# A two-layer hybrid attention kernel: the memory keys normed from unscaled rows, only the values scaled

## The chip, the cores and the metric

The kernel runs on one core of a Trainium2 chip. The metric is the time of one execution on the device in microseconds (us); the lower the better. The core has TensorE (PE: matrix products and transpositions; its weight loads have a row of their own, PEld), VectorE (DVE), ScalarE (ACT), GpSimd (POOL) and SyncE (SP), whose queue issues nearly all transfers here.

## The reference

Two layers, each with 256 tokens of 1024 columns. In each layer the tokens are normed and projected; three kinds of attention run (causal over one block, 6 heads; dilated, 6 heads; over 256 rows of a memory, 4 heads); each output is gated, and one projection brings all back to 1024 columns. What the change touches is the memory's side:

```python
def rms_norm(x, g):
    xf = x.astype(jnp.float32)
    y = xf * lax.rsqrt(jnp.mean(xf * xf, axis=-1, keepdims=True) + EPS)
    return (y * g.astype(jnp.float32)).astype(x.dtype)
...
    mkv = jnp.einsum('bmd,de->bme', rms_norm(mem, mem_norm_g), w_mem_kv)
    m_k, m_v = jnp.split(mkv, 2, axis=-1)
    qm = rms_norm(to_heads(m_q, N_HEADS_MEM), qk_g[4])
    km = rms_norm(to_heads(m_k, N_HEADS_MEM), qk_g[5])
    om = from_heads(memory_attention(qm, km, to_heads(m_v, N_HEADS_MEM)))
```

The factor r = rsqrt(mean(mem²) + EPS) of a memory row is one number for the row, so it may be put on after the projection; and a key's own norm, over the 64 columns of a head, is taken of the row with r in it.

## The kernel before

All weights come in fp32 and are split into two parts, `hi` (a cast on ScalarE) and `lo` (raw less `hi`, on VectorE); a product is three matrix products (`hi`·`xmh`, `hi`·`xml`, `lo`·`xmh`), added in PSUM. Each weight arrives in a `raw` tile (3 buffers), and each piece of it becomes one `hi` and one `lo` (5 buffers of each). The projections follow one another on TensorE in a written order: memory keys and values (`mkv`), memory queries (`mq`), their gate (`mg`), then the dilated heads' `bq`, `bk`, `bv` and so on. Each projection has two accumulators of PSUM, `acc`, in a ring of four: `bq` takes the two that `mq` had, so its second accumulator is free only when VectorE has read the second row of `mq` (the product by the gain in `normed`, line 266).

Attention runs as tasks beside the projections: a planner on the host writes each task's TensorE instructions between those of the projections by planned times, and that order is fixed. The first task on TensorE transposes one pair of memory heads (`qn` and `kn`, 128 rows of tokens and of memory at a time: q0, k0, q1, k1, line 113) in the middle of `bq`, after five of its eight steps.

`normed` is the norm of heads: squares on ScalarE (`sq`, 260), their sums on VectorE (`hss`, 262), mean plus EPS on VectorE (`ms`, 154), the power of -1/2 on GpSimd (`hrs`, 155), the product by the gain (`t1`, 266) and by the norm (276), both on VectorE. `row_scale` gives a row's factor: squares of 1024 columns with their sum on ScalarE (160), `ms` on VectorE, the power on GpSimd.

In layer 0 `mkv` ends before the factors `rmem` are there. So the rows are copied out of PSUM unscaled (`kv`, 561); the squares of memory row tile 0 follow in the middle of `mq` (564), those of tile 1 after `mq`'s norm (568); and each row tile of keys and values (512 columns) is scaled in place on ScalarE (573) before the keys' norm (574). A row tile here is 128 memory rows. Layer 1 has the factors at hand and scales in the copy.

Within an engine, the instructions of this part stand in an order that a scheduler settles when the program is built, from planned times; on the chip each engine then goes through its own list in that order.

Of the kernel before, what the change touches and what calls it, by code (L numbers as in the profile page):

```python
# [10 lines left out]
F32 = mybir.dt.float32  # L11
F32R = mybir.dt.float32r
AF = mybir.ActivationFunctionType
ALU = mybir.AluOpType
AX = mybir.AxisListType

P = 128
T = 256
NT = T // P
D = 1024  # L20
KD = D // P
HD = 64
# [44 lines left out]
def hybrid_kernel(ctx: ExitStack, tc: tile.TileContext, x, mem, mem_t, gains, w_in, w_out, w_mem_kv, qk_g, const, out):  # L67
    nc = tc.nc
    cp = ctx.enter_context(tc.tile_pool(name="cp", bufs=1))
    wp = ctx.enter_context(tc.tile_pool(name="wp", bufs=2))  # L70
    sp = ctx.enter_context(tc.tile_pool(name="sp", bufs=2))
# [17 lines left out]
    def pin(ins):  # L89

        return tc.keep_in_program_order(ins) if pinning[0] else ins

    memT = cp.tile([P, KD, T], F32, name="memT")
    mem_sb = cp.tile([P, NT, D], F32, name="mem_sb")
# [29 lines left out]
    def poll():  # L124

        for task in list(tasks):
            if task[0] <= clock[0]:
                try:
                    task[0] = next(task[1]) + clock[0]
                except StopIteration:  # L130
                    tasks.remove(task)
# [20 lines left out]
    def rsqrt(dst, ss, n, scale):  # L152
        ms = sp.tile([P, n], F32, tag="ms", name="ms", bufs=4)
        pin(nc.vector.tensor_scalar(ms, ss, scale, EPS, op0=ALU.mult, op1=ALU.add))  # L154
        pin(nc.gpsimd.tensor_tensor(dst, ms, mhalf[:, :n], op=ALU.pow))  # L155

    def row_scale(src, t, name, junk):

        ss = sp.tile([P, 1], F32, tag="ss", name="ss", bufs=4)
        pin(nc.scalar.activation(junk, src[:, t], AF.Square, accum_out=ss))  # L160
        r = sp.tile([P, 1], F32, tag=name, name=name, bufs=2)
        rsqrt(r, ss, 1, 1.0 / D)
        return r
# [26 lines left out]
    gB = cp.tile([P, DEPTH, 6, HD], F32, name="gB")  # L190

    def load_gains(a, b):
        pin(nc.sync.dma_start(gB[:, :, a:b], bass.AP(tensor=qk_g.tensor, offset=qk_g.offset + a * HD,
                                                     ap=[[0, P], [6 * HD, DEPTH], [HD, b - a], [1, HD]])))
# [57 lines left out]

    def heads(v):
        return v.rearrange("p (h d) -> p h d", d=HD)

    def normed(acc, n, dst, tables):

        h = n // HD
        sq = sp.tile([P, n], F32, tag="sq", name="sq", bufs=2)
        pin(nc.scalar.activation(sq, acc, AF.Square))  # L260
        ss = sp.tile([P, h], F32, tag="hss", name="hss", bufs=4)
        pin(nc.vector.tensor_reduce(ss, heads(sq), axis=AX.X, op=ALU.add))  # L262
        rs = sp.tile([P, h], F32, tag="hrs", name="hrs", bufs=4)
        rsqrt(rs, ss, h, 1.0 / HD)
        t1 = sp.tile([P, n], F32, tag="t1", name="t1", bufs=2)
        pin(nc.vector.tensor_tensor(heads(t1), heads(acc), tables[0][:, None, :].to_broadcast([P, h, HD]),
                                    op=ALU.mult))
        if len(tables) > 1:
            t2 = sq
            half = dict(s=2, d=HD // 2)  # L270
            pin(nc.vector.tensor_tensor(t2.rearrange("p (h s d) -> p h s d", **half),
                                        acc.rearrange("p (h s d) -> p h s d", **half)[:, :, ::-1, :],
                                        tables[1].rearrange("p (s d) -> p s d", s=2)[:, None]
                                        .to_broadcast([P, h, 2, HD // 2]), op=ALU.mult))
            pin(nc.vector.tensor_tensor(t1, t1, t2, op=ALU.add))
        pin(nc.vector.tensor_tensor(heads(dst), heads(t1), rs.unsqueeze(2).to_broadcast([P, h, HD]), op=ALU.mult))  # L276
# [97 lines left out]
    for i, (l, c) in enumerate(order):  # L374
        if c in e_rows:
            e0, n = e_rows[c]
            units += [(i, a, min(2, n - a), D) for a in range(0, n, 2)]
        else:
            n = 512 if c == "mkv" else in_cols[c][1]
# [101 lines left out]
    for l in range(DEPTH):  # L481
# [3 lines left out]
        if l == 0:  # L485
# [4 lines left out]
            r_mem = []  # L490
# [44 lines left out]
        def head_tiles(n, nv):  # L535
            return [sp.tile([P, NT, n], F32, tag=c, name=c, bufs=1) for c in ("qn", "kn")] + [
                sp.tile([P, NT, nv], F32, tag="v", name="v", bufs=2),
                sp.tile([P, n // P, T], F32, tag="gate", name="gate", bufs=2)]
# [14 lines left out]
        qn, kn, kv, gate = head_tiles(256, 512)  # L553
        v = kv[:, :, 256:512]
        ready = dict(gate=1e9)
        mq, steps = project(xs, weights(), 256)
        for i, _ in enumerate(steps):
            poll()
            if i == 0:
                for t in range(NT):  # L560
                    pin(nc.scalar.activation(kv[:, t], mkv[t], AF.Copy, **(dict(scale=r_mem[t]) if r_mem else {})))
            if i == 3 and l == 0:
                mem_junk = sp.tile([P, D], F32, tag="v", name="mem_junk", bufs=2)
                r_mem.append(row_scale(mem_sb, 0, "rmem", mem_junk))
        for t, acc in enumerate(mq):
            normed(acc, 256, qn[:, t], [gB[:, l, 4]])
        if l == 0:
            r_mem.append(row_scale(mem_sb, 1, "rmem", mem_junk))
            pin(nc.sync.dma_start(cst, const))
            load_gains(0, 4)  # L570
        for t in range(NT):
            if l == 0:
                pin(nc.scalar.activation(kv[:, t], kv[:, t], AF.Copy, scale=r_mem[t]))
            normed(kv[:, t, 0:256], 256, kn[:, t], [gB[:, l, 5]])
        pinning[0] = False
        start_heads(2, 6, qn, kn, None, v, gate, ready, D_NORM + D_MEM)
        tab = prepare_tables(l)
# [3 lines left out]
        for kind, e0 in ((2, 3), (0, 0)):  # L581
# [7 lines left out]
            qn, kn, v, gate = head_tiles(384, 384)  # L589
# [75 lines left out]
```

## Time and profile before

| | |
|---|---|
| time, median of 3 runs | 294.21 us (294.15 to 294.81) |
| the profiled execution's own time | 294.36 us |
| its span, first to last instruction | 292.6 us |
| TensorE busy | 285.8 us, 98% of the span |
| VectorE busy | 204.3 us, 70% |
| ScalarE busy | 200.0 us, 68% |
| GpSimd busy | 53.8 us, 18% |
| granted clock of TensorE | 1.000 in the mean |

The 1.76 us between the span and the time of that execution lie outside what the profile shows. A busy share is a mean over the whole span; where an engine stands idle for a moment is read from the views below.

### The profile page before, as it was taken

The page shows a single profiled execution, that of the slowest core. Times are in us where ns is not written, and L with a number is a line of the kernel's source. Part 1 is how long each engine was busy: PE and PEld are TensorE (multiplying, and loading weights), DVE is VectorE, ACT ScalarE, POOL GpSimd, SP SyncE. Part 2 cuts the span into 40 slices and gives each one's busy share as a digit, 9 for nine tenths or more (in the row PEclk, how much of TensorE's full clock was granted, in tenths as well). Part 3 has the DMA queues.
Part 4 walks back from the last instruction along what each step waited for, and adds up shares of the span by engine and source line. Part 5 has one row for each costly group of instructions (what it writes and reads, how often), then busy time and mean ns, then how long its engine had stood idle before and what let it go on. Part 6 is the DMA issues. An engine that isn't in the chain of part 4 may idle for free.

```text
span 292.6 us, 4974 instructions
## 1 busy us (share of the span) xinstructions
PE 285.8 (98%) x1810; PEld 250.6 (86%) x1810; DVE 204.3 (70%) x456; ACT 200.0 (68%) x445; POOL 53.8 (18%) x73
## 2 busy tenths in 40 slices
PE   8999889999999999999999999999999999999994
PEld 5699879889988999877788999989899899987773
DVE  1696889796557997755585577979655699765413
ACT  2997858785798747978375655868588864698600
POOL 0103596030002130000011049703000123000000
PEclk9999999999999999999999999999999999999999
DMA  7999565609227046646106727560913715820003
GB/s 236 389 367 373 184 182 186 179 2 319 57 71 237 19 155 262 196 162 224 65 19 233 225 101 195 168 179 2 298 38 109 239 52 165 316 81 36 3 0 143
DMA packets 32793, 47.33 MB, mean 162 GB/s; under 512 B 1280, under 2 KB 27648, under 8 KB 32768
## 3 DMA queue, kind: packets, MB, share of 16 engines
q1 hardware_dynamic: 32336, 46.22, 48.5%
q10 hardware_dynamic: 432, 0.79, 0.8%
q8 instruction: 14, 0.23, 0.3%
q14 instruction: 11, 0.09, 0.1%
HBM read 45.96 MB, written 1.05 MB: 161 GB/s over the span
## 4 chain that ended last, share of the span: by engine, by line
PE 86%; DMA 7%; DVE 3%; POOL 1%; issue 1%; ACT 1%; SPq 0%; DVEq 0%; ACTq 0%
PE acc L110 68%; PE wk L113 7%; PE wk L110 5%; PE o L110 5%; DMA raw<-in_w_in_dram 3%; DMA x_sb<-in_x_dram 2%; DVE lo L430 1%; DMA raw<-in_w_mem_kv_dram 1%; POOL hrs L155 1%; DVE hss L262 0%; ACT xn L160 0%; POOL r L155 0%; DVE ms L154 0%; DVE kn L276 0%; ACT hi L429 0%
## 5 line engine op out<-in xcount | busy, mean ns | idle before, releaser
L430 DVE TENSOR_TENSOR lo<-raw,hi 128x768 fp32r<-128x768 f32 (+1 forms) x91 | 97.4, 1089 | 34.1 <-ACT hi L429 33.4
L429 ACT CAST hi<-raw 128x768 fp32r<-128x768 f32 (+1 forms) x91 | 83.8, 937 | 31.2 <-PE acc L110 22.7
L110 PE MATMUL acc<-hi,xmh 128*128 128x384 f32 (+2 forms) x252 | 67.3, 349 | 0.8 <-ACT hi L429 0.8
L110 PE MATMUL acc<-hi,xml 128*128 128x384 f32 (+2 forms) x252 | 63.6, 335 | 0.0
L110 PE MATMUL acc<-lo,xmh 128*128 128x384 f32 (+2 forms) x252 | 63.6, 335 | 0.0
L155 POOL TENSOR_TENSOR hrs<-ms,mhalf 128x6 f32<-128x6 f32 (+1 forms) x24 | 30.1, 1255 | 121.2 <-DVE ms L154 120.8
L110 PEld LDWEIGHTS acc<-hi,xmh 128*128 128x128 f32 x252 | 42.7, 189 | 6.3 <-issue 3.0
L110 PEld LDWEIGHTS acc<-lo,xmh 128*128 128x128 f32 x252 | 45.0, 188 | 1.2
L110 PEld LDWEIGHTS acc<-hi,xml 128*128 128x128 f32 x252 | 44.9, 188 | 1.2
L110 PE MATMUL acc<-hi,yT 128*128 128x512 f32 x128 | 41.0, 402 | 0.0
L110 PE MATMUL acc<-xmh,hi 128*128 128x256 f32 x128 | 29.7, 293 | 0.0
L340 ACT ACTIVATE pr<-pr,nm 128x128 f32<-128x128 f32 (+1 forms) x48 | 21.4, 447 | 11.1 <-DVE nm L338 10.9
L110 PE MATMUL acc<-xmh,lo 128*128 128x256 f32 x128 | 28.4, 283 | 0.0
L110 PE MATMUL acc<-xml,hi 128*128 128x256 f32 x128 | 28.4, 283 | 0.0
L110 PEld LDWEIGHTS acc<-hi,yT 128*128 128x128 f32 x128 | 23.0, 188 | 4.9 <-issue 0.7
L346 ACT ACTIVATE pr<-pr,rinv 128x128 f32<-128x128 f32 (+1 forms) x64 | 25.8, 462 | 0.2 <-DVE rinv L344 0.2
L110 PE MATMUL acc<-lo,yT 128*128 128x512 f32 x64 | 25.0, 391 | 0.0
L110 PEld LDWEIGHTS acc<-xmh,hi 128*128 128x128 f32 x128 | 20.9, 191 | 0.7 <-issue 0.7
L110 PEld LDWEIGHTS acc<-xml,hi 128*128 128x128 f32 x128 | 21.0, 191 | 0.0
L110 PEld LDWEIGHTS acc<-xmh,lo 128*128 128x128 f32 x128 | 21.0, 191 | 0.0
L357 ACT COPY pT<-wk 128x384 f32<-128x384 f32 (+1 forms) x32 | 15.5, 504 | 5.1 <-PE wk L113 5.1
L338 DVE CUSTOM_DVE_ANT_0 pr<-wk,cst 128x128 f32<-128x128 f32 (+1 forms) x48 | 14.2, 352 | 3.0 <-PE wk L110 3.0
(76 smaller groups left out, 355.3 us busy)
## 6 DMA issues: line engine op xcount, KB each, us to landing
raw<-in_w_in_dram SPq DMA_DIRECT2D x24, 768.0 KB, 4.8
raw<-in_w_in_dram SPq DMA_DIRECT2D x7, 1024.0 KB, 5.4
raw<-in_w_out_dram SPq DMA_DIRECT2D x6, 1024.0 KB, 4.9
raw<-in_w_in_dram SPq DMA_DIRECT2D x6, 512.0 KB, 3.7
raw<-in_w_out_dram SPq DMA_DIRECT2D x4, 512.0 KB, 4.2
raw<-in_w_mem_kv_dram SPq DMA_DIRECT2D x2, 1024.0 KB, 5.3
raw<-in_w_mem_kv_dram SPq DMA_DIRECT2D x2, 512.0 KB, 6.5
x_sb<-in_x_dram SPq DMA_DIRECT2D x2, 512.0 KB, 6.7
```

Of the source, the lines that this page charges most:

```text
L110: pe(nc.tensor.matmul(out, a, b, start=start, stop=stop), us)
L113: pe(nc.tensor.transpose(out, a, ident), 0.109)
L155: pin(nc.gpsimd.tensor_tensor(dst, ms, mhalf[:, :n], op=ALU.pow))
L338: nc.vector.tensor_tensor_reduce(out=pr[:, spans[t]], in0=s[:, spans[t]], in1=masks[t], scale=-1.0, scalar=3e38, op0=ALU.add, op1=ALU.min, ...
L340: nc.scalar.activation(pr[:, spans[t]], pr[:, spans[t]], AF.Exp, scale=-1.0, bias=nm[:, t:t + 1], accum_out=sums[:, t:t + 1])
L346: nc.scalar.activation(pr[:, spans[t]], pr[:, spans[t]], AF.Copy, scale=rinv[:, t:t + 1])
L357: nc.scalar.copy(pT[:, :n], ps[:, :n])
L429: pin(nc.scalar.copy(hi, raw))
L430: pin(nc.vector.tensor_tensor(lo, raw, hi.bitcast(F32), op=ALU.subtract))
```

## The change

In layer 0 the keys are normed from the unscaled rows. Right after the copy out of PSUM, ScalarE squares the keys' 256 columns of both row tiles and VectorE sums them (`head_squares`); the two row tiles' own squares (1024 columns each) follow at once. The norm's end, `normed_keys`, forms r²/64 (`r2`), puts it into `ms` as the factor of the sums, and multiplies the unscaled keys by r and by the gain in one instruction. The two scalings in place take the values' 256 columns alone. Layer 1 is as before.

```diff
+    def head_squares(acc, n):
+        sq = sp.tile([P, n], F32, tag="sq", name="sq", bufs=2)
+        pin(nc.scalar.activation(sq, acc, AF.Square))
+        ss = sp.tile([P, n // HD], F32, tag="hss", name="hss", bufs=4)
+        pin(nc.vector.tensor_reduce(ss, heads(sq), axis=AX.X, op=ALU.add))
+        return ss
+
+    def normed_keys(acc, ss, r, dst, table):
+        h = 256 // HD
+        r2 = sp.tile([P, 1], F32, tag="r2", name="r2", bufs=2)
+        pin(nc.vector.tensor_scalar(r2, r, r, 1.0 / HD, op0=ALU.mult, op1=ALU.mult))
+        rs = sp.tile([P, h], F32, tag="hrs", name="hrs", bufs=4)
+        rsqrt(rs, ss, h, r2)
+        t1 = sp.tile([P, 256], F32, tag="t1", name="t1", bufs=2)
+        pin(nc.vector.scalar_tensor_tensor(heads(t1), heads(acc), r, table[:, None, :].to_broadcast([P, h, HD]),
+                                           op0=ALU.mult, op1=ALU.mult))
+        pin(nc.vector.tensor_tensor(heads(dst), heads(t1), rs.unsqueeze(2).to_broadcast([P, h, HD]), op=ALU.mult))
...
             if i == 3 and l == 0:
+                k_ss = [head_squares(kv[:, t, 0:256], 256) for t in range(NT)]
                 mem_junk = sp.tile([P, D], F32, tag="v", name="mem_junk", bufs=2)
-                r_mem.append(row_scale(mem_sb, 0, "rmem", mem_junk))
+                r_mem += [row_scale(mem_sb, t, "rmem", mem_junk) for t in range(NT)]
         for t, acc in enumerate(mq):
             normed(acc, 256, qn[:, t], [gB[:, l, 4]])
         if l == 0:
-            r_mem.append(row_scale(mem_sb, 1, "rmem", mem_junk))
             pin(nc.sync.dma_start(cst, const))
             load_gains(0, 4)
         for t in range(NT):
             if l == 0:
-                pin(nc.scalar.activation(kv[:, t], kv[:, t], AF.Copy, scale=r_mem[t]))
-            normed(kv[:, t, 0:256], 256, kn[:, t], [gB[:, l, 5]])
+                normed_keys(kv[:, t, 0:256], k_ss[t], r_mem[t], kn[:, t], gB[:, l, 5])
+                pin(nc.scalar.activation(v[:, t], v[:, t], AF.Copy, scale=r_mem[t]))
+            else:
+                normed(kv[:, t, 0:256], 256, kn[:, t], [gB[:, l, 5]])
```

The scheduler orders each engine's list anew. TensorE's and SyncE's lists stay the same. The list of ScalarE from the copies out of PSUM on, before (a number behind a name tells buffers apart; `acc_260` and `acc_261` are the two rows of `mq`, `raw_262` and `raw_305` the first and second half of `bq`'s weights):

```order
L561 ACTIVATE v_258<-acc_127 128x512
L561 ACTIVATE v_258<-acc_128 128x512
L160 ACTIVATE mem_junk_298,ss_299<-mem_sb_84 128x1024
L429 CAST hi_307<-raw_262 128x768
L260 ACTIVATE sq_335<-acc_260 128x256
L260 ACTIVATE sq_346<-acc_261 128x256
L160 ACTIVATE mem_junk_298,ss_357<-mem_sb_84 128x1024
L573 ACTIVATE v_258<-v_258,rmem_301 128x512
L429 CAST hi_410<-raw_262 128x768
L260 ACTIVATE sq_366<-v_258 128x256
L429 CAST hi_440<-raw_305 128x768
```

And with the change:

```order
L581 ACTIVATE v_258<-acc_127 128x512
L581 ACTIVATE v_258<-acc_128 128x512
L259 ACTIVATE sq_298<-v_258 128x256
L259 ACTIVATE sq_302<-v_258 128x256
L160 ACTIVATE mem_junk_306,ss_307<-mem_sb_84 128x1024
L160 ACTIVATE mem_junk_306,ss_313<-mem_sb_84 128x1024
L449 CAST hi_321<-raw_262 128x768
L280 ACTIVATE sq_349<-acc_260 128x256
L280 ACTIVATE sq_360<-acc_261 128x256
L594 ACTIVATE v_258<-v_258,rmem_309 128x256
L594 ACTIVATE v_258<-v_258,rmem_315 128x256
L449 CAST hi_414<-raw_262 128x768
L449 CAST hi_444<-raw_319 128x768
```

The keys' squares and both rows' squares now stand ahead of the first cast of `bq`'s weights, and behind it stand the queries' squares and the two scalings of values.

The list of VectorE around the second row of `mq`, before; the product `t1_354<-acc_261` is what frees the second accumulator of `bq`:

```order
L262 TENSOR_REDUCE hss_348<-sq_346 128x4
L154 TENSOR_SCALAR ms_351<-hss_348 128x4
L266 TENSOR_TENSOR t1_354<-acc_261,gB_95 128x256
L430 TENSOR_TENSOR lo_411<-raw_262,hi_410 128x768
L276 TENSOR_TENSOR qn_256<-t1_354,hrs_350 128x256
L154 TENSOR_SCALAR ms_360<-ss_357 128x1
L262 TENSOR_REDUCE hss_368<-sq_366 128x4
L430 TENSOR_TENSOR lo_441<-raw_305,hi_440 128x768
```

And with the change, where that product is `t1_368<-acc_261`:

```order
L282 TENSOR_REDUCE hss_362<-sq_360 128x4
L450 TENSOR_TENSOR lo_415<-raw_262,hi_414 128x768
L154 TENSOR_SCALAR ms_365<-hss_362 128x4
L286 TENSOR_TENSOR t1_368<-acc_261,gB_95 128x256
L450 TENSOR_TENSOR lo_445<-raw_319,hi_444 128x768
L296 TENSOR_TENSOR qn_256<-t1_368,hrs_364 128x256
```

The second `lo` of `bq`, which stood behind that product, now stands ahead of it, and the third `lo` ahead of the norm's end `qn`.

The list of VectorE from there to the end of the second key row, before (`gate` are the two products of `mg`'s gate):

```order
L430 TENSOR_TENSOR lo_441<-raw_305,hi_440 128x768
L154 TENSOR_SCALAR ms_371<-hss_368 128x4
L266 TENSOR_TENSOR t1_374<-v_258,gB_95 128x256
L533 SCALAR_TENSOR_TENSOR gate_259<-th_468,acc_408 128x256
L276 TENSOR_TENSOR kn_257<-t1_374,hrs_370 128x256
L262 TENSOR_REDUCE hss_380<-sq_378 128x4
L533 SCALAR_TENSOR_TENSOR gate_259<-th_471,acc_409 128x256
L154 TENSOR_SCALAR ms_383<-hss_380 128x4
L266 TENSOR_TENSOR t1_386<-v_258,gB_95 128x256
L430 TENSOR_TENSOR lo_481<-raw_305,hi_480 128x768
L276 TENSOR_TENSOR kn_257<-t1_386,hrs_382 128x256
```

And with the change:

```order
L268 TENSOR_SCALAR r2_373<-rmem_309 128x1
L553 SCALAR_TENSOR_TENSOR gate_259<-th_472,acc_412 128x256
L154 TENSOR_SCALAR ms_376<-hss_300,r2_373 128x4
L272 SCALAR_TENSOR_TENSOR t1_379<-v_258,rmem_309,gB_95 128x256
L553 SCALAR_TENSOR_TENSOR gate_259<-th_475,acc_413 128x256
L274 TENSOR_TENSOR kn_257<-t1_379,hrs_375 128x256
L268 TENSOR_SCALAR r2_383<-rmem_315 128x1
L450 TENSOR_TENSOR lo_485<-raw_319,hi_484 128x768
L154 TENSOR_SCALAR ms_386<-hss_304,r2_383 128x4
L272 SCALAR_TENSOR_TENSOR t1_389<-v_258,rmem_315,gB_95 128x256
L450 TENSOR_TENSOR lo_503<-raw_442,hi_502 128x768
L274 TENSOR_TENSOR kn_257<-t1_389,hrs_385 128x256
```

The keys' sums `hss` have left this stretch, two `r2` of one column have come in, and the first `lo` of `bk` (`lo_503`, before `lo_499`) now stands ahead of the last `kn`.

## Rows read from the trace of the kernel before

**Rows 1.** The page's first line: the span of the profiled execution.
```profile
span 292.6 us, 4974 instructions
```

**Rows 2.** All waits of TensorE: engine, line, releaser, us in total, times, longest.
```profile
PE warm L120 <- DVE mhalf L83: 1.0, 1, 1.0
PE wk L113 <- DVE kn L276: 0.9, 1, 0.9
PE acc L110 <- ACT hi L429: 0.8, 1, 0.8
PE acc L110 <- DVE whole L495: 0.4, 1, 0.4
```

**Rows 3.** Timeline of TensorE: start us, us, engine, line, operation, tiles, count, idle before.
```profile
30.91 0.34 PE L110 MATMUL acc<-hi,xmh 128*128 128x384 f32 x1
32.01 0.41 PE L110 MATMUL acc<-hi,xmh 128*128 128x384 f32 x1 [0.77 <-ACT hi L429]
...
37.11 0.27 PE L113 MATMUL wk<-ident,qn 128*128 128x128 f32 x1
...
37.33 0.27 PE L113 MATMUL wk<-ident,qn 128*128 128x128 f32 x1
38.55 0.33 PE L113 MATMUL wk<-ident,kn 128*128 128x128 f32 x1 [0.95 <-DVE kn L276]
```

**Rows 4.** Timeline of VectorE from 27.96 to 45 us.
```profile
27.96 0.96 DVE L430 TENSOR_TENSOR lo<-raw,hi 128x768 fp32r<-128x768 f32 x1 [2.71 <-ACT hi L429]
...
30.58 0.42 DVE L276 TENSOR_TENSOR qn<-t,hrs 128x256 f32<-128x256 f32 x1 [0.79 <-POOL hrs L155]
30.92 0.41 DVE L262 TENSOR_REDUCE hss<-sq 128x4 f32<-128x256 f32 x1
31.37 0.17 DVE L154 TENSOR_SCALAR ms<-hss 128x4 f32<-128x4 f32 x1
31.45 0.42 DVE L266 TENSOR_TENSOR t<-acc,gB 128x256 f32<-128x256 f32 x1
31.78 0.94 DVE L430 TENSOR_TENSOR lo<-raw,hi 128x768 fp32r<-128x768 f32 x1
32.66 0.43 DVE L276 TENSOR_TENSOR qn<-t,hrs 128x256 f32<-128x256 f32 x1
33.00 0.15 DVE L154 TENSOR_SCALAR ms<-ss 128x1 f32<-128x1 f32 x1
33.07 0.41 DVE L262 TENSOR_REDUCE hss<-sq 128x4 f32<-128x256 f32 x1
33.39 0.95 DVE L430 TENSOR_TENSOR lo<-raw,hi 128x768 fp32r<-128x768 f32 x1
...
37.06 0.95 DVE L430 TENSOR_TENSOR lo<-raw,hi 128x768 fp32r<-128x768 f32 x1
38.03 0.46 DVE L276 TENSOR_TENSOR kn<-t,hrs 128x256 f32<-128x256 f32 x1
...
44.98 1.28 DVE L331 TENSOR_REDUCE nm<-wk 128x2 f32<-128x512 f32 x2
```

**Rows 5.** Timeline of ScalarE from 22.82 us.
```profile
22.82 1.14 ACT L561 ACTIVATE v<-acc 128x512 f32<-128x512 f32 x2
23.79 1.12 ACT L160 ACTIVATE mem_junk<-mem_sb 128x1024 f32<-128x1024 f32 x1
24.73 0.26 ACT L160 ACTIVATION_READ_ACCUMULATOR mem_junk<-mem_sb 128x1 f32 x1
27.09 0.83 ACT L429 CAST hi<-raw 128x768 fp32r<-128x768 f32 x1 [2.10 <-DMA raw<-in_w_in_dram]
...
44.08 0.83 ACT L429 CAST hi<-raw 128x768 fp32r<-128x768 f32 x1 [0.84 <-DMA raw<-in_w_in_dram]
```

**Rows 6.** Timeline of GpSimd, two of the norms' powers.
```profile
31.61 1.01 POOL L155 TENSOR_TENSOR hrs<-ms,mhalf 128x4 f32<-128x4 f32 x1 [1.07 <-DVE ms L154]
...
36.89 1.11 POOL L155 TENSOR_TENSOR hrs<-ms,mhalf 128x4 f32<-128x4 f32 x1 [1.27 <-DVE ms L154]
```

## The prediction

> **What bounds the kernel now.** I read the page first: the span is 292.6 us [rows 1] and TensorE is busy for nearly all of it, so a microsecond taken from another engine is worth nothing unless TensorE waits for it. The second view is therefore the list of TensorE's own waits [rows 2]. It has four entries, 3.1 us together. Two belong to the start-up (`warm` and `whole`), which the change doesn't touch. The other two, 0.8 and 0.9 us, lie in layer 0 just where the change works. TensorE's list is the same before and after, and behind the second of these waits the view has none up to the end of the span. So whatever TensorE is late or early behind that point is carried to the end one to one, and the prediction is the question when TensorE passes it.
>
> The third view is the timeline of TensorE there [rows 3]. The first wait ends at 32.01, when the product into the second accumulator of `bq` begins. The view puts it down to a cast on ScalarE. But the matrix product needs the same weights as the one at 30.91 that had begun already; what differs is the accumulator, which VectorE frees by the product that runs from 31.45 for 0.42 us, to 31.87 [rows 4]. I take that as the releaser, with 0.14 us from its end to TensorE's start. The second wait ends at 38.55: the fourth transposition of the first memory pair needs the second row tile of `kn`, whose last step runs on VectorE from 38.03 for 0.46 us [rows 3, 4]. The third transposition starts at 37.33, and the first three are 0.11 apart, so TensorE could have started the fourth at 37.44: 1.11 us are lost there.
>
> Both waits hang on VectorE's list from 27.96 on, so the fourth view is its timeline [rows 4], with the powers on GpSimd that it waits for [rows 6].
>
> **The change part by part.**
>
> *ScalarE ahead of the first `bq` cast.* Before, one pass of 1024 columns and its read stand between the copies and the wait for a transfer: 23.79 to 24.99, 1.20 us; then ScalarE is idle for 2.10 us until the weights land and the cast starts at 27.09 [rows 5]. Now two squares of 256 columns and two such passes stand there. The two copies of 512 columns are 0.97 us apart from the next instruction, so two passes of half that width cost no more than 0.97; two passes with their reads cost 2.40. The block ends at 27.16 at the latest. If the squares cost half of the bound it ends at 26.7, inside the idle time. I take 0 for it; the bound is 0.07 us late. On VectorE the two sums of keys and two `ms` fall into its own idle 2.71 us before 27.96 [rows 4]: 0.41 each and 0.15 each, 1.1 us, and the first power on GpSimd follows in that gap too. So `lo` starts at 27.96 as before, and everything up to the reduction at 30.92 is unchanged.
>
> *VectorE from 30.92 on.* I step through the new list with start-to-start times of rows: a reduction 0.32 (33.07 to 33.39), `ms` 0.08 (31.37 to 31.45), a pass of 256 columns 0.33 (31.45 to 31.78), `qn` 0.34 (32.66 to 33.00), `lo` 0.88 (31.78 to 32.66), a one-column instruction 0.07 (33.00 to 33.07) [rows 4]. A power on GpSimd starts 0.24 after its `ms` (31.37 to 31.61), takes 1.01 to 1.11, and `kn` starts 0.03 after it [rows 4, 6].
>
> The reduction at 30.92 is followed by `lo` at 31.24, `ms` at 32.12, and the product that frees the accumulator at 32.20, against 31.45 before: 0.75 us later, because an 0.88 us `lo` now stands ahead of it (less 0.13 of the reduction's latency, which it covers). So TensorE's first wait ends at 32.76 instead of 32.01, and its steps up to the third transposition arrive 0.75 later: it could start the fourth at 38.19.
>
> Behind it: `lo` 32.53, `qn` 33.41 (its power runs 32.36 to 33.37, hidden under `lo`), `r2` 33.75, `gate` 33.82, `ms` 34.15, keys times r and gain 34.23, `gate` 34.56. `kn` waits for its power, 34.39 to 35.50, and starts at 35.53. Then `r2` 35.87, `lo` 35.94, `ms` 36.82, keys 36.90, `lo` 37.23 to 38.11. The second power runs from 37.06 to 38.17, and the last `kn` starts at 38.20 instead of 38.03: 0.17 us later. The instruction with r and gain in it isn't in the trace; I cost it as the 256-column product it replaces, since it makes one pass over the same columns. Bounds: the same 0.33, or as much as two passes (0.66); of that, 0.33 at the second key row would lie under the power, so it would move little.
>
> The casts that feed the two earlier `lo` are ready: ScalarE has lost a 1.20 us pass from the stretch where the second and third cast stand, while their `lo` come 0.54 (31.24 against 31.78) and 0.86 (32.53 against 33.39) earlier.
>
> *What is taken away.* Half the columns of two scalings, the keys' squares behind them and one row's squares leave ScalarE's stretch between 27 and 35 us. None of it stood on TensorE's path except through `kn`, and there the chain over GpSimd's factor, the scaling, the squares and the sums was hidden by other entries of VectorE's list: without it, the list is still full to 38.2. The saved chain thus pays only for one `lo` of `bk` that was moved ahead of `kn`.
>
> *The sum.* First wait +0.75; second wait: TensorE reaches it at 38.19 and goes on at 38.20 + 0.52 = 38.72, against 38.55. Net +0.17 us: the wait moves from the second place to the first, and TensorE comes out as late as before. The profiled execution takes 294.36, which makes 294.53; it stands 0.15 above the median of the runs, 294.21, so the median becomes **294.4 us**. A change within 0.3% (0.88 us) counts as none; the runs shown spread by 0.66 us.
>
> *A rule against it.* Pairs of `lo` and power stand close together at both places: before, `lo` started 0.17 us behind a power (37.06 against 36.89), and it kept its usual 0.95 us and ended by 38.01 [rows 4, 6]. The Trainium skill, page SBUF — State Buffer, section "SBUF: two separate sides", says that a VectorE instruction with two inputs in SBUF and a GpSimd instruction that reads SBUF take a shared port pair by turns, and that the one that starts first holds it to its end. By that, `lo` would have started at 38.00; the row disagrees, so the sum goes by the row.
>
> **The rivals.**
> *A small gain.* If the last `kn` comes early, TensorE no longer waits at the second place at all. But it can't be there before 38.19, since the accumulator still holds it 0.75 us; so the most is 38.55 - 38.19 = 0.36 us: a median of 293.85. For it speaks that each of the 16 steps was read from one execution; against it that VectorE's list would have to be 0.5 us shorter than the rows add up to.
>
> *A large gain* would have to come from a wait other than the two, and [rows 2] have none; I keep a little for what I can't see: 293.2.
>
> *A transfer behind `bq`.* Before, the first cast of `bv` waits for its weights until 44.08 [rows 5], and the squares of `bq` stand ahead of it; now it stands ahead of them, and its `lo` ahead of the softmax's first `nm`, which before began at 44.98 [rows 4]. If the weights land no earlier, `nm` begins at 44.08 + 0.83 + 0.04 + 0.88 = 45.83, 0.85 late. The weights' buffer comes free about 1.1 us earlier, though (a `lo` that started at 37.06 now does at 35.94), so they should land earlier. At worst +0.85 on top of the sum: 295.2.
>
> *Slower: `lo` and power by turns.* If a power holds off the `lo` behind it, the third `lo` waits from 32.53 to 33.37 and the fifth until its power ends: 0.84 us each, and `kn` is 0.17 + 2 x 0.84 = 1.85 late: 296.1. It decides from one such hold on (1.0 us). This is what that page's rule would do; the row at 37.06 speaks against it.
>
> *Slower: ScalarE's block ends late.* VectorE's list hangs on the first cast at 27.09; each 0.1 us by which the block overruns is 0.1 us on TensorE. From 0.7 late on, it decides. The bound by rows is 0.07, so it would need passes a fifth slower than that bound has them: 295.1.
>
> **How the numbers follow.** The forecast 0.53; the small gain 0.17; a large gain 0.08; the transfer 0.07; `lo` and power by turns 0.04; the late block, or another entry of VectorE's list that is late by 0.7 or more, 0.11. Faster by over 0.3%: 0.08. Slower by over 0.3%: the last two, 0.15. The rest, 0.77, is no difference. The range runs from 293.7 (below the small gain) to 295.2 (the transfer and the start of the late block).
>
> **What would show it.** TensorE's first wait grows from 0.77 to about 1.5 us and its releaser is VectorE's product by the gain, with a `lo` ahead of it; the second shrinks from 0.95 to some 0.4; the fourth transposition starts near 38.7. ScalarE still waits for the transfer ahead of its first `bq` cast. The forecast is wrong if that cast starts after 27.2, if a third wait of TensorE appears behind 39 us, or if the last `kn` starts before 37.7 or after 38.9.

## The result: slower by half a per cent, and the profile after

The changed kernel takes 295.9 us in the median of 6 runs (295.67 to 296.36), the kernel before 294.52 on the same chip (294.15 to 294.81, 6 runs). The ratio is 1.0052, with a 95% interval of 1.004 to 1.0065. The forecast was 294.4 with a range from 293.7 to 295.2; the measured time lies above it. The second comparison of the changed kernel, told below, leaves out one execution of six that took 562.08 us at the full granted clock; its cause isn't known. The profiled execution took 295.91 us, and its span is 1.5 us longer than in [rows 1]. The first line of its page:

```profile
span 294.1 us, 4977 instructions
```

The waits of TensorE (engine, line, releaser, us in total, times, longest), to be held against [rows 2]:

```profile
PE wk L113 <- DVE kn L274: 1.6, 1, 1.6
PE acc L110 <- DVE t L286: 1.4, 1, 1.4
```

The first wait has nearly doubled, as forecast, and its releaser is now named as VectorE's product by the gain. The second should have shrunk to some 0.4 and has grown to 1.6. TensorE's timeline (start us, us, engine, line, operation, tiles, count, idle before), against [rows 3]:

```profile
31.31 0.34 PE L110 MATMUL acc<-hi,xmh 128*128 128x384 f32 x1
33.10 0.41 PE L110 MATMUL acc<-hi,xmh 128*128 128x384 f32 x1 [1.45 <-DVE t L286]
...
40.28 0.33 PE L113 MATMUL wk<-ident,kn 128*128 128x128 f32 x1 [1.56 <-DVE kn L274]
```

The fourth transposition starts 1.73 us later than before; the first product of `bq`, ahead of both waits, was already 0.40 late (31.31 against 30.91). The other waits of its list belong to the start, up to 9.71 us; there is none behind these two. What lies behind is carried along nearly unchanged: from the start of the fourth transposition to the end of the span it is 253.8 to 254.1 us in all the traces, before and after and in every experiment. VectorE's timeline, against [rows 4]; the tile `r` of line 268 is the program's `r2`:

```profile
28.30 0.96 DVE L450 TENSOR_TENSOR lo<-raw,hi 128x768 fp32r<-128x768 f32 x1 [0.92 <-ACT hi L449]
...
31.60 0.95 DVE L450 TENSOR_TENSOR lo<-raw,hi 128x768 fp32r<-128x768 f32 x1
32.47 0.16 DVE L154 TENSOR_SCALAR ms<-hss 128x4 f32<-128x4 f32 x1
32.54 0.41 DVE L286 TENSOR_TENSOR t<-acc,gB 128x256 f32<-128x256 f32 x1
...
34.68 0.48 DVE L272 SCALAR_TENSOR_TENSOR t<-v,rmem,gB 128x256 f32<-128x256 f32 x1
35.07 0.41 DVE L553 SCALAR_TENSOR_TENSOR gate<-th,acc 128x256 f32<-128x256 f32 x1
...
36.39 0.21 DVE L268 TENSOR_SCALAR r<-rmem 128x1 f32<-128x1 f32 x1
36.52 0.95 DVE L450 TENSOR_TENSOR lo<-raw,hi 128x768 fp32r<-128x768 f32 x1
37.38 0.23 DVE L154 TENSOR_SCALAR ms<-hss,r 128x4 f32<-128x4 f32 x1
37.52 0.48 DVE L272 SCALAR_TENSOR_TENSOR t<-v,rmem,gB 128x256 f32<-128x256 f32 x1
37.91 0.96 DVE L450 TENSOR_TENSOR lo<-raw,hi 128x768 fp32r<-128x768 f32 x1
39.77 0.46 DVE L274 TENSOR_TENSOR kn<-t,hrs 128x256 f32<-128x256 f32 x1 [0.90 <-POOL hrs L155]
```

And the keys' two powers on GpSimd, against the second of [rows 6]:

```profile
34.85 1.17 POOL L155 TENSOR_TENSOR hrs<-ms,mhalf 128x4 f32<-128x4 f32 x1 [1.13 <-DVE ms L154]
37.69 2.04 POOL L155 TENSOR_TENSOR hrs<-ms,mhalf 128x4 f32<-128x4 f32 x1 [1.67 <-DVE ms L154]
```

Most of the time went here. The second power took 2.04 us where 1.11 were forecast, and VectorE stood idle for 0.90 us ahead of the last `kn`, with nothing else to wait for. The power began 0.22 before `lo`, `lo` ran its usual 0.96 to 38.87, and the power ended at 39.73, 0.86 us after that. Before, it ended at 38.00 in [rows 6], about when `lo` did; but that too is 0.86 after the end of another VectorE instruction, the keys' product, which ends at 36.72 + 0.42 = 37.14. VectorE's row of before:

```profile
36.72 0.42 DVE L266 TENSOR_TENSOR t<-v,gB 128x256 f32<-128x256 f32 x1
```

In both traces the power looks as if it did its work only when a VectorE instruction with two SBUF inputs had ended: the product before, `lo` after. The first key power of the changed kernel fits: behind its product stands a `gate`, which has one input in PSUM, and the power ends 0.86 after the product (36.02 after 34.68 + 0.48). So does the queries' power in [rows 6], whose product reads PSUM: it takes 1.01 from its own start, though a `lo` starts 0.17 behind it. GpSimd's spans in a profile are rough, so the offsets count here, and that they repeat.

Because the start of an execution varies, the clean measure is the length of VectorE's chain from the start of `bq`'s first `lo` to that of the last `kn`. Before it was 38.03 - 27.96 = 10.07. The forecast steps make 10.24. After, it is 39.77 - 28.30 = 11.47: 1.40 longer, close to the 1.38 between the medians.

### The profile page after: what moved, and what is told of

Same layout as the page of the kernel before. It is cut to its first block, busy times and chain, and to the rows that moved or that the text cites. A ratio compares the mean times of both kernels' runs of the same rounds, so it can differ in the third digit from the quotient of the medians.

```text
span 294.1 us, 4977 instructions
## 1 busy us (share of the span) xinstructions
PE 285.3 (97%) x1810; PEld 250.1 (85%) x1810; DVE 204.9 (70%) x458; ACT 199.8 (68%) x445; POOL 55.0 (19%) x73
## 4 chain that ended last, share of the span: by engine, by line
PE 85%; DMA 7%; DVE 2%; POOL 2%; issue 2%; ACT 1%; SPq 0%; DVEq 0%; POOLq 0%; ACTq 0%
PE acc L110 68%; PE wk L113 7%; PE wk L110 5%; PE o L110 5%; DMA raw<-in_w_in_dram 3%; DMA x_sb<-in_x_dram 2%; POOL hrs L155 2%; DMA raw<-in_w_mem_kv_dram 1%; DVE lo L450 1%; ACT xn L160 0%; POOL r L155 0%; ACT hi L449 0%; DVE ms L154 0%; DVE xml L185 0%; DVE hss L282 0%
## 5 line engine op out<-in xcount | busy, mean ns | idle before, releaser
L155 POOL TENSOR_TENSOR hrs<-ms,mhalf 128x6 f32<-128x6 f32 (+1 forms) x24 | 31.4, 1307 | 121.1 <-DVE ms L154 120.8
```

## The experiments

Each kernel below was timed beside the kernel before on the same chip. "Chain" is the length just defined, "power" the second key power; both are read from one profiled execution of each kernel. The last version has another list, in which neither has a counterpart.

| kernel | chain | power | ratio to before (95%) |
|---|---|---|---|
| before | 10.07 | 1.11 | |
| changed | 11.47 | 2.04 | 1.0052 (1.004 to 1.0065) |
| changed, again | 11.47 | 2.04 | 1.0057 (1.0045 to 1.0069) |
| `lo`s of `bk` behind the last `kn` | 10.59 | 1.17 | 1.0021 (1.0005 to 1.0037) |
| that `lo` in halves | 11.06 | 1.64 | 1.0041 (1.0027 to 1.0056) |
| keys' product without r | 10.35 | 1.11 | 1.0031 (1.0016 to 1.0045) |
| before, product with a column | 10.20 | 1.17 | 1.0007 (0.9992 to 1.0021) |
| second `lo` behind the product | 10.81 | 2.04 | 1.0039 (1.0025 to 1.0054) |
| second row's squares back | 10.78 | 2.04 | 1.0032 (1.0019 to 1.0045) |
| before, second row's squares early | 10.76 | 1.11 | 1.0032 (1.002 to 1.0043) |
| squares back, product without r | 9.73 | 1.11 | 0.9997 (0.9985 to 1.0008) |
| products first | | | 0.9956 (0.9944 to 0.9968) |

**Does `lo` hold the power?** First, the changed kernel with `bk`'s `lo`s (and those after them) ordered behind the last `kn`. `behind` puts one instruction after another in its engine's list, and `marks["kn"]` is the last `kn`:

```diff
...
-            pin(nc.vector.tensor_tensor(lo, raw, hi.bitcast(F32), op=ALU.subtract))
+            ins = pin(nc.vector.tensor_tensor(lo, raw, hi.bitcast(F32), op=ALU.subtract))
+            if s >= 12 and "kn" in marks:
+                behind(ins, marks["kn"])
```

> The changed kernel, with the `lo` of bk's first half (and those after it) placed behind the last `kn` on VectorE, so that nothing runs on VectorE beside the second key row's power. Theory 1 (that `lo` holds the power off): the power falls from 2.04 to 1.1 to 1.2 us, the last `kn` starts about 0.9 us earlier, TensorE's second wait falls from 1.56 to about 0.7, and the time falls by 0.9 us, to about 295.0. Theory 2 (the power is slow by itself, since its input comes from an instruction with a pointer, or for its place behind another power): it still takes about 2.0 us and the time stays at 295.9. First wait in both: 1.45.

It took 295.04 us against 294.36, as the first theory had it. The power took 1.17 and the chain fell by 0.88. TensorE's second wait fell to 0.72. The first is 1.10 where 1.45 was expected; the second run of the changed kernel shows 1.13. It varies with how far TensorE is ahead of VectorE in an execution when it comes to `bq`; the `lo` ahead of the product is untouched.

Second, the same `lo` cut in two, one half ahead of `kn` and one behind it:

```diff
-            pin(nc.vector.tensor_tensor(lo, raw, hi.bitcast(F32), op=ALU.subtract))
+            for h in ([slice(0, 1), slice(1, 2)] if s == 12 else [slice(0, nk)]):
+                pin(nc.vector.tensor_tensor(lo[:, h], raw[:, h], hi[:, h].bitcast(F32), op=ALU.subtract))
```

> The changed kernel, with that one `lo` in two instructions of half the columns; the first half stands ahead of the last `kn`, the second behind it. Theory 1 (the power is held until the VectorE instruction beside it ends): the hold is halved, the power takes 1.5 to 1.6 us, the last `kn` starts 0.4 to 0.5 us earlier and the time falls by about 0.45 us, to 295.4. Theory 2 (slow by itself): 2.0 us and 295.9.

Its VectorE timeline:

```profile
38.30 0.55 DVE L451 TENSOR_TENSOR lo<-raw,hi 128x384 fp32r<-128x384 f32 x1
39.75 0.46 DVE L274 TENSOR_TENSOR kn<-t,hrs 128x256 f32<-128x256 f32 x1 [0.90 <-POOL hrs L155]
```

And GpSimd's:

```profile
38.07 1.64 POOL L155 TENSOR_TENSOR hrs<-ms,mhalf 128x4 f32<-128x4 f32 x1 [1.67 <-DVE ms L154]
```

The half `lo` ends at 38.85 and the power at 39.71, again 0.86 later; the median was 295.62 us, where 295.4 was expected. The power's length follows `lo`'s end, so `lo` holds it. The Trainium skill, page SBUF — State Buffer, section "SBUF: two separate sides", has a VectorE instruction with two SBUF inputs and a GpSimd instruction that reads SBUF exclude one another, the one that starts first going on to its end. These rows agree as far as the power is held by `lo`. The other direction isn't seen: a `lo` behind a power that had started ran its usual time in every trace here, also behind one that was not held at all (0.94 from 31.78, beside the 1.01 from 31.61, [rows 4, 6]). Here the measurement decides: what the trace shows as the start of a power doesn't tell which of the two goes first.

**Why here, and not before?** Ahead of the power now stand an `ms` and a product that read one column per row (a pointer operand). The changed kernel with a product without r; the row's mean square goes into the sums instead, still as a column of `ms`. With it `r2` loses its column too, since it is now a multiple of that mean square by a constant:

```diff
-        pin(nc.vector.tensor_scalar(r2, r, r, 1.0 / HD, op0=ALU.mult, op1=ALU.mult))
+        pin(nc.vector.tensor_scalar(r2, r, EPS * HD, 1.0, op0=ALU.mult, op1=ALU.mult))
...
-        rsqrt(rs, ss, h, r2)
+        ms = sp.tile([P, h], F32, tag="ms", name="ms", bufs=4)
+        pin(nc.vector.tensor_scalar(ms, ss, r2, 1.0 / HD, op0=ALU.add, op1=ALU.mult))
+        pin(nc.gpsimd.tensor_tensor(rs, ms, mhalf[:, :h], op=ALU.pow))
...
-        pin(nc.vector.scalar_tensor_tensor(heads(t1), heads(acc), r, table[:, None, :].to_broadcast([P, h, HD]),
-                                           op0=ALU.mult, op1=ALU.mult))
+        pin(nc.vector.tensor_tensor(heads(t1), heads(acc), table[:, None, :].to_broadcast([P, h, HD]), op=ALU.mult))
```

> The changed kernel, with the keys' product as a plain tensor_tensor by the gain (the row's factor goes into the norm instead: the sums plus EPS times the row's mean square, so the result is the same); the order of all lists is that of the changed kernel. Theory 1a (any `lo` that starts while the power has not yet read holds it, and the order of the list decides): the power stays at about 2.0 us, time 295.9. Theory 1b (the product with a pointer is longer, 0.48 against 0.42, and hands VectorE over to `lo` without a gap into which the power comes): the power falls to 1.1 us and the time to about 295.0.

Its second product and the `lo` behind it on VectorE:

```profile
37.22 0.42 DVE L277 TENSOR_TENSOR t<-v,gB 128x256 f32<-128x256 f32 x1
37.56 0.95 DVE L454 TENSOR_TENSOR lo<-raw,hi 128x768 fp32r<-128x768 f32 x1
```

And the power on GpSimd:

```profile
37.39 1.11 POOL L275 TENSOR_TENSOR hrs<-ms,mhalf 128x4 f32<-128x4 f32 x1 [1.61 <-DVE ms L274]
```

The power took 1.11 beside a whole `lo`, in the same place of the list; the median was 295.33, where 295.0 was expected. So with this `ms` the forms decide: the product's, as long as `r2`, which stands one `lo` earlier, has no part in it. The reverse, the kernel before with a column of ones in the keys' product:

```diff
-            normed(kv[:, t, 0:256], 256, kn[:, t], [gB[:, l, 5]])
+            normed(kv[:, t, 0:256], 256, kn[:, t], [gB[:, l, 5]], None if l else ones[:, 0:1])
```

> The kernel before, with the keys' product of layer 0 as scalar_tensor_tensor with a column of ones as its pointer; all else and all lists as before. Theory 1b (the pointer form closes the gap): the power of the second key row rises from 1.11 to about 2.0 us, the last `kn` comes 0.9 us later and the time rises to about 295.4. Theory 1a (the list decides, not the form): the power stays at 1.1 to 1.2 us and the time at 294.5 to 294.6.

On VectorE and on GpSimd:

```profile
36.72 0.48 DVE L272 SCALAR_TENSOR_TENSOR t<-v,ones,gB 128x256 f32<-128x256 f32 x1
37.12 0.95 DVE L435 TENSOR_TENSOR lo<-raw,hi 128x768 fp32r<-128x768 f32 x1
...
36.90 1.17 POOL L157 TENSOR_TENSOR hrs<-ms,mhalf 128x4 f32<-128x4 f32 x1 [1.27 <-DVE ms L156]
```

The power took 1.17 and wasn't held by `lo`; the median was 294.6. The theory that the product's form alone decides falls. Among the kernels of the table with a `lo` right behind the product, it held the power in those where both `ms` and the product had a column, and in none where one of them had it or neither. Next, the changed kernel with `bq`'s second `lo` put behind the product that frees the accumulator, so that another `lo` stands beside the power:

```diff
+            if s == 9:
+                behind(ins, marks["product"])
```

> The changed kernel, with the second `lo` of bq behind the product that frees bq's second accumulator, as it stood before the change. The scheduler then puts the fourth `lo` of bq (which waits for TensorE alone) between the second key product and the last `kn`, and the `lo` of bk (which waits for a transfer, TensorE and ScalarE) behind it. First wait of TensorE in every theory: back from 1.45 to about 0.8. If the pointer forms of the product and of `ms` are what lets a `lo` in ahead of the power: the power is held again, 2.0 us, and the last `kn` starts about as late as in the changed kernel; time 295.5 to 295.9, since the second wait takes up what the first gives. If it also takes the `lo` of bk: the power takes 1.17 us and the time is that of the kernel before or a little less, 294.0 to 294.6.

The first wait fell to 0.36, further than expected, since TensorE came to `bq` 1.25 later than before (32.16) and VectorE to its first `lo` 0.85 later. But the scheduler now had the fourth `lo` of `bq` between the second keys' product and the last `kn`, and the power took 2.04 again: it needn't be a `lo` of `bk`. The median was 295.82. The changed kernel itself, run once more:

> The changed kernel once more. If the hold is settled by the lists and forms, the power of the second key row takes 2.04 us again, with the same offsets; if it is a toss-up between runs, it may take 1.17, and the time would lie between 295.0 and 295.9. Time otherwise 295.9 against 294.4 to 294.5.

The power took 2.04 and the chain 11.47, as in the first run of this kernel (295.56 to 296.75 us without the one execution named above): the hold repeats.

**What each part of the change costs.** The second memory row's squares, put back behind the queries' norm in the changed kernel, and moved early in the kernel before:

```diff
-                r_mem += [row_scale(mem_sb, t, "rmem", mem_junk) for t in range(NT)]
+                r_mem.append(row_scale(mem_sb, 0, "rmem", mem_junk))
...
+            r_mem.append(row_scale(mem_sb, 1, "rmem", mem_junk))
```

> The changed kernel, but the second memory row's squares stand behind the queries' norm again, as before the change. VectorE's list then has the product that frees bq's accumulator ahead of its `lo` again, one `lo` stands between the second keys' product and the last `kn`, and ScalarE's block ahead of the first bq cast is 1.2 us shorter. Theory (the pointer `ms` and pointer product together let the next `lo` hold the power; the rest is order): the first wait is 0.77 as before; the second key power starts about 8.7 us after the first bq `lo` starts and takes about 2.0; the last `kn` starts 10.75 after that `lo` (before: 10.07, after: 11.47); the fourth transposition 0.7 later than before; median 295.1, and it spreads no more than before, since the cast waits for the transfer again. Rival (the hold needs the order of after, with two `lo` ahead): the power takes 1.17, `kn` starts 9.9 after the first `lo`, median 294.2. Rival (ScalarE's block has no part in the medians): the median lies 0.4 or more above the profiled shift.

The median was 295.3 us against 294.37. Its GpSimd timeline:

```profile
36.62 2.04 POOL L155 TENSOR_TENSOR hrs<-ms,mhalf 128x4 f32<-128x4 f32 x1 [1.13 <-DVE ms L154]
```

And VectorE's:

```profile
27.91 0.96 DVE L450 TENSOR_TENSOR lo<-raw,hi 128x768 fp32r<-128x768 f32 x1 [1.85 <-ACT hi L449]
...
36.84 0.95 DVE L450 TENSOR_TENSOR lo<-raw,hi 128x768 fp32r<-128x768 f32 x1
38.69 0.46 DVE L274 TENSOR_TENSOR kn<-t,hrs 128x256 f32<-128x256 f32 x1 [0.90 <-POOL hrs L155]
```

The chain is 10.78 where 10.75 was expected: the power is held without the order of the changed kernel too. TensorE's first wait shows 0.48, not 0.77. The other way round, the kernel before with only these squares moved (the diff above with its signs turned):

> The kernel before, with one part of the change alone: the second memory row's squares follow the first row's; scaling of keys and values and the keys' norm as before, in plain forms. VectorE's list gets two `lo` ahead of the queries' last steps, as in after. Theory: the first wait grows by 0.75 to about 1.5; the second key power is not held (1.11); the sums of the keys stay in the list, so the last `kn` starts 10.74 after the first `lo` (before 10.07), the fourth transposition is 0.67 later, median 295.1. Rival (two `lo` ahead are what makes the power lose): power 2.0, `kn` 11.6 after the first `lo`, median 296.0. Rival (the order costs nothing, all comes from the keys' norm): 294.4.

The chain is 10.76 where 10.74 was expected, the power 1.11, the median 295.27. So the early squares cost 0.69 us of chain by themselves, through the order of VectorE's list; with the 0.71 of the run above that makes the 1.40. Two numbers missed: TensorE's first wait shows 0.48, not 1.5, and the fourth transposition is 0.25 late, not 0.67, since in this execution TensorE itself came 0.60 later to `bq` and VectorE 0.43 earlier. With both remedies, squares back and the product without r:

> The changed kernel with both remedies: the second memory row's squares behind the queries' norm as before, and the keys' product and mean in the forms that were not held (product without the column r; the row's mean square put into the sums instead). Theory: the power takes 1.11; VectorE's list has lost two sums of 0.32 and gained two one-column instructions of 0.13 and two longer `ms`, so the last `kn` starts 9.8 after the first `lo` (before 10.07); first wait 0.77, second about 0.7; the fourth transposition 0.25 earlier than before, median 294.15. Rival (something else of the change costs time): 294.8 or more.

The median was 294.24 us against 294.37, and the chain 9.73: shorter than before by 0.34 (0.25 to 0.3 expected). TensorE's first wait shows 1.16, not 0.77, because TensorE came to `bq` 0.43 earlier (30.48). In this list the chain holds no cost of the change any more, and what it saves there can't be told from nothing in the median.

**A better list.** From the version without r in the product: the queries' gain products ahead of their norm, which frees the accumulators, the keys' powers begun early, all products by the norm at the end, and two `lo` behind the queries' last `ms` (their casts behind the queries' last squares; `t1` has four buffers instead of two):

```diff
...
+                pin(nc.vector.tensor_tensor(heads(t1), heads(acc),
+                                            gB[:, l, 4][:, None, :].to_broadcast([P, 256 // HD, HD]), op=ALU.mult))
...
+            for k in keys + queries:
+                scaled(*k)
...
+            if s in (9, 10):
+                behind(ins, marks["mean"])
```

> A version made to remove both waits: the queries' products by the gain stand ahead of their norm, so that bq's second accumulator is free before TensorE comes to it; the keys' powers are begun in VectorE's idle time before 28 us (the row's mean square takes the factor's place, so they need no factor from GpSimd); the second and third `lo` of bq stand behind the queries' last `ms` (the scheduler puts them behind both `kn` and both `qn`). If the two waits are what TensorE loses here, both vanish: 0.77 + 1.11 = 1.9 us under the kernel before, 292.5 to 292.8. If another wait takes their place (the softmax of the first memory pair, for which TensorE now comes 1.9 us earlier, or the weights of bk), up to 1 us of it is given back: 293.5.

It took 292.98 us (292.83 to 293.77) against 294.46, and beats both kernels. TensorE's timeline:

```profile
34.74 0.62 PE L110 MATMUL acc<-lo,xmh 128*128 128x384 f32 x2 [0.34 <-DVE lo L467]
...
37.61 0.27 PE L113 MATMUL wk<-ident,kn 128*128 128x128 f32 x1
```

Both waits are gone: the fourth transposition starts 0.94 us earlier than before, without a wait. That it isn't the 1.9 of the two waits goes with two things in this trace: TensorE came to `bq` 0.55 later than before (31.46), and there is a new wait of 0.34 at a delayed `lo`. The median lies 0.2 above the expectation; the new wait may be why.

## Why the prediction was wrong

**Right:** the reading of the two waits as what decides, and of the first one's releaser. The releaser that the list of waits names can't decide this: it is a cast on ScalarE before and in the second run of the changed kernel, and the product in the first. The offset does: in all ten traces in which TensorE waits there, it goes on 0.14 to 0.15 after the product's end. On VectorE the product starts 4.24 after `bq`'s first `lo` (32.54 - 28.30), where it was 3.49 (31.45 - 27.96): 0.75 more, as the step said. The moves of the lists were right too, and so was the reasoning that TensorE carries whatever it is late by to the end, to within 0.3 us (the 253.8 to 254.1 above). Two of the signs of being wrong came true: the first cast of `bq` starts at 27.44, after 27.2, and the last `kn` at 39.77, after 38.9.

**The step that failed:** "The second power runs from 37.06 to 38.17". It took a duration from a row where the power stood beside a `lo` and wasn't held by it, and put it beside instructions of another form. It measured 2.04 in place of 1.11, because a `lo` held the power to its end: the sum had 0.93 us too little.

**Mis-sized:** the one-column and pointer forms (a pointer form reads one column per row as an operand). The two `r2` stand 0.13 from start to start, not 0.07; `ms` with a column takes 0.23 and its power starts 0.31 after it, not 0.24; the product with r takes 0.48 and 0.39 from start to start, not 0.33, inside the bounds given (0.33 to 0.66). Of these 0.22 reach the second `ms` and 0.07 its power: 0.3 in all. The three pieces, 0.17 as forecast, 0.93 and 0.30, make the 1.40.

**The rival "`lo` and power by turns"** had the right two instructions and came to 296.1, but with the roles turned round: it let the power hold `lo`, and was set aside with a chance of 0.04 because the row at 37.06 in [rows 4] showed `lo` unheld. That its time is near the measured 295.9 is luck: it has two holds of 0.84 on `lo`, and there was one of 0.93 on the power. That row could speak only of that direction. For the other, rows of before were there to be read, on GpSimd a little further on:

```profile
40.51 1.03 POOL L206 TENSOR_TENSOR tab<-gB,cst 128x64 f32<-128x64 f32 x1
...
42.51 0.32 POOL L206 TENSOR_TENSOR tab<-gB,cst 128x64 f32<-128x64 f32 x1
```

The same line's product takes 1.03 while VectorE works through `lo`s (VectorE's last of four ends at 42.36) and 0.32 when it doesn't. So GpSimd's instructions were longer beside `lo`s in the kernel before already, and the power of 1.11 could have been read as a shorter one (1.01 in [rows 6]) behind something.

**ScalarE's block** was forecast to end at 26.7 to 27.16, hidden by the wait for the transfer. In the changed kernel's profile it ends at 27.20:

```profile
23.22 1.15 ACT L581 ACTIVATE v<-acc 128x512 f32<-128x512 f32 x2
...
27.01 0.19 ACT L160 ACTIVATION_READ_ACCUMULATOR mem_junk<-mem_sb 128x1 f32 x1
27.44 0.83 ACT L449 CAST hi<-raw 128x768 fp32r<-128x768 f32 x1 [0.24 <-DVE ms L154]
```

Its length was right: from the copies to the end of the block it is 3.98, where 26.7 to 27.16 less 22.82 makes 3.9 to 4.3. What the step left out is that the copies' start varies between executions, and the block now fills the idle time that took this up. The run with the column of ones, which has the block of before, against the run with the halved `lo`, which has the longer one. ScalarE's timeline of the first:

```profile
23.77 1.14 ACT L566 ACTIVATE v<-acc 128x512 f32<-128x512 f32 x2
...
27.03 0.83 ACT L434 CAST hi<-raw 128x768 fp32r<-128x768 f32 x1 [1.08 <-DMA raw<-in_w_in_dram]
```

And of the second:

```profile
23.96 1.14 ACT L582 ACTIVATE v<-acc 128x512 f32<-128x512 f32 x2
...
27.84 0.82 ACT L449 CAST hi<-raw 128x768 fp32r<-128x768 f32 x1
```

Copies 1 us late left the cast where it was (27.03, 27.09 in [rows 5]) with the short block, and made it 0.75 late with the long one. How much of the medians this is, the runs don't settle. The changes of the medians lie 0.1 to 0.3 above the changes of the chain for most kernels, 0.6 to 0.7 for two with the long block (product without r, second `lo` behind the product), but not at all for the changed kernel in its first comparison.

**Still open:** why the hold came only with both pointer forms, and whether these alone decide. The version without r in the product changed `r2` as well, and the column of ones stood in the kernel before, with its list. In the trace the power, the product and `lo` stand to one another in the run with the column of ones as they do in the changed kernel (the power 0.18 and 0.17 after the product's start, `lo` 0.22 after the power's in both), and one power is held and the other isn't. Where in the two forms the turn is decided, no run here shows.

## What to carry to other kernels

A duration read from a trace has its neighbours in it: ask of each instruction on the path what stands beside it in the new list, in both directions, and look for the same instruction elsewhere in the trace, alone and in company. Work taken off an engine that wasn't waited for buys nothing, while the order in which a scheduler refills that engine's list can cost more than the work. A long instruction that nobody needs soon (`lo` of the next projection) belongs behind the instructions that free an accumulator or feed a transposition. Idle time ahead of a transfer may be what keeps a late start from spreading; the two executions compared above suggest it and don't prove it.

## What the hardware showed that I had not expected

The second key power on GpSimd ended 0.86 to 0.87 us after a VectorE instruction with two SBUF inputs in eleven traces: the product where `lo` didn't hold it (38.00 after 37.14 before), else the half `lo` (39.71 after 38.85) or the whole one (39.73 after 38.87). And a VectorE instruction with a one-column operand took some 0.06 us more than the same without: `ms` 0.22 to 0.23 against 0.16 to 0.17, the product 0.48 against 0.42.
